# Context's modulation vectors on GpSimd, a third pair by seven products, one vector in the second mixer

## The chip, the cores and the metric

The kernel runs on one core of a Trainium2 chip. PE is the matrix engine, DVE the vector engine, ACT the scalar engine, POOL is GpSimd, and SP is the queue that issues most DMAs. The metric is the device time of one execution in microseconds. Before the change it is 2030.13 us (median of three runs, 2025.8 to 2033.44).

## The reference, cut to what matters

Two layers run over 256 latent tokens and 256 context tokens of width 1024:

```
m  = (silu(c)     @ w_ada[l] + b_ada[l])     # nine vectors of 1024 for the latent tokens
mc = (silu(c_ctx) @ w_ada[l] + b_ada[l])     # the same nine for the context
x  = x  + 0.5*m[2] *swiglu(modulate(rms_norm(x),  m[0],  m[1]),  w1, w3, w2)    # first FFN
y  = token_mixer(modulate(rms_norm(x), m[3], m[4]), ...);  x = x + m[5]*y
x  = x  + 0.5*m[8] *swiglu(modulate(rms_norm(x),  m[6],  m[7]),  w1, w3, w2)    # second FFN
...                                           # the context stream the same with mc; in the last
                                              # layer it ends after the first FFN
swiglu(h, w1, w3, w2) = (silu(h @ w1) * (h @ w3)) @ w2                           # hidden width 2816
```

## The kernel before

**Products.** Activations lie with channels on the 128 partitions and tokens along the row, latent in columns 0 to 255 and context in 256 to 511. Each fp32 operand is split into two fp32r halves (`split_act`: ACT copies the high half, DVE subtracts it for the low half), and three matmuls (high x high, high x low, low x high) make one product. `load_raw` brings 128x1024 floats of weights into a ring `wr` of five tiles.

**An FFN over both streams** (`ffn_both`, called three times: layer 0 twice, layer 1 once) takes the hidden width in eleven pairs of 256 channels. An ordinary pair is four units (two halves of w1, two of w3), each 24 matmuls of 512 columns. A pair "by seven products" (`seven`) has seven units of 24 matmuls of 256 columns, on sums of blocks of weights and of activations; `Forms` makes the sums of activations. Its tiles `s1` and `s3` are each loaded by SP and then added to by a second, accumulating DMA that POOL issues (L759). Pair 0 comes with the handover from the stage before, pairs 1 and 2 are ordinary, 3 to 10 go by seven. Behind pairs 3, 7 and 10 stand the down-projections of what is finished, in units of up to 24 matmuls of 512 columns.

**The order** on PE, DVE and ACT is the order of the code (`pipeline`): at each unit the evacuations of the unit before, the weight split of the unit three ahead, then the unit's matmuls. POOL and SP are ordered by the scheduler. A queue that waits holds up all behind it.

**The modulation vectors** (`ada`) are made beside this: one step loads 128x1024 of `w_ada` into the ring and adds it, times a scalar per partition, to two accumulators in one tile `aacc`, for the latent and the context stream, both on DVE (L238 the first step, L240 the others). After eight steps `ada_end` sums over partitions on PE (`pa`, L255), copies to `mrow` on DVE, transposes on PE (L262) and adds the bias. There is one tile `aacc`, so the first step of a vector waits until PE has read the one before. `pipeline` spreads the steps by each unit's `cost`: 1 for the ordinary units of pair 2, 1 at one unit of a pair by seven, 0.22 per four-row block of the down-projections. One vector, (1,7), goes another way: `ada_apart` multiplies by `w_ada` on PE in the third of these FFNs (L279), between ordinary units. In the mixers and the last FFN the steps are taken by `tick` and `background`.

Of the kernel before, what the change touches and what calls it, by code (L numbers as in the profile page):

```python
# [17 lines left out]
P = 128  # L18
# [61 lines left out]
def dit_kernel(ctx: ExitStack, tc: tile.TileContext, I: dict, out: bass.AP):  # L80
# [146 lines left out]
    def ada(mods, pool, made=None):  # L227
# [22 lines left out]
    def ada_end(l, m, acc, pool):  # L250
# [3 lines left out]
        for q in range(4):  # L254
            te.matmul(pa[32 * q:32 * q + 32, 0, :], ones32, acc[:, q % 2, (q // 2) * 512:(q // 2 + 1) * 512],  # L255
                      start=True, stop=True, tile_position=(0, 32 * q))
# [11 lines left out]
        modulated(l, m)  # L268

    def ada_apart(l, m, pool, made):  # L270

        pa = psum_bg(f"pa{l}_{m}")
        v.memset(pa[:, 0, 0:L], 0.0)
        ahead = ada_load(l, m, 0)
        yield
        for k in range(KD):
            w, ahead = ahead, ada_load(l, m, k + 1) if k + 1 < KD else None
            for q in range(4):
                te.matmul(pa[32 * q:32 * q + 2, 0, 0:L], cs[:, k], w[:, q * L:(q + 1) * L],  # L279
                          start=(k == 0), stop=(k == KD - 1), tile_position=(0, 32 * q))  # L280
            if k == KD - 1:
                made.append(ada_apart_end(l, m, pa, pool))
            yield

    def ada_apart_end(l, m, pa, pool):
        mrow = pool.tile([P, 512], F32, tag="mrow", name="mrow")[:, 0:L]
        v.tensor_copy(mrow, pa[:, 0, 0:L])
        yield
        for b in range(2):
            te.transpose(pa[:, 1, b * P:(b + 1) * P], mrow[:, b * P:(b + 1) * P], ident)  # L290
        yield
        v.tensor_tensor(modT[l][:, m].rearrange("p (q b) t -> p q b t", q=4),
                        pa[:, 1, 0:L].rearrange("p (b q r) -> p q b r", b=2, q=4)[:, :, :, 0:2],
                        biasT[l][:, 8 * m:8 * m + 8].rearrange("p (q b) -> p q b", q=4).unsqueeze(3)
                        .to_broadcast([P, 4, 2, 2]), ALU.add)
        modulated(l, m)
# [353 lines left out]
    def pipeline(units, fills, steps, total, made, apart):  # L650
# [17 lines left out]
        with tc.manual_schedule(engines={eng.PE, eng.DVE, eng.Activation}):  # L668
            for i in range(len(units) + 1):
                prev = units[i - 1] if i else None  # L670
                if prev:
                    if prev.need is not None:
                        while did < prev.need and step():
                            did += 1
                        finish(True)
# [19 lines left out]
                if i < len(units):  # L695
                    want += units[i].cost * scale
                    while did < min(total, int(want + 1e-6)) and step():
                        did += 1
                    for _ in range(2):
                        next(apart, None)  # L700
# [5 lines left out]
    class Forms:  # L706


        def __init__(self, norm, fp):
# [8 lines left out]
            t.append(fp.tile([P, 2, D], F32, tag="aacc", name="ft")[:, 0].rearrange("p (k n) -> p k n", k=4))  # L718

            def whole(o, a, b):  # L720
                v.tensor_tensor(o, a.bitcast(F32), b.bitcast(F32), ALU.add)

            def neg(a, b):
# [848 lines left out]
```

## Time and profile before

| | |
|---|---|
| median of three runs | 2030.13 us |
| the profiled execution's own time | 2027.78 us |
| its span | 2025.9 us |
| PE busy | 1943.0 us (96%) |
| DVE busy | 1556.6 us (77%) |
| ACT busy | 965.5 us (48%) |
| POOL busy | 117.6 us (6%) |
| mean granted clock of PE | 0.982 |

Shares are means over stages with different limits. A DVE busy for 77% of the span can still be the last to be ready in one stage, so the stages are read one by one.

### The profile page before, as it was taken

What the parts mean: (1) busy time and instruction counts of PE and PEld (TensorE: products, weight loads), DVE (VectorE), ACT (ScalarE), POOL (GpSimd) and SP (SyncE); (2) the same over time, 40 slices, a digit from 0 to 9 for tenths busy, and PEclk for the clock granted to TensorE, in tenths of its full rate; (3) what the DMA queues carried; (4) which work ended last, traced back from release to release, by engine and by line L of the source; (5) the groups of instructions that cost most, each with busy time, mean ns of one, the idle gap of its engine ahead of it and who ended that gap; (6) DMA issues with size and microseconds to landing.
All of it is one profiled execution on the core that took longest, in us unless ns stands there. A gap on an engine that the chain in (4) does not pass through costs nothing. (4 is left out here: it accounts for less than half of the span.)

```text
span 2025.9 us, 32128 instructions
## 1 busy us (share of the span) xinstructions
PE 1943.0 (96%) x12797; PEld 1730.5 (85%) x12797; DVE 1556.6 (77%) x2323; ACT 965.5 (48%) x1466; POOL 117.6 (6%) x80
## 2 busy tenths in 40 slices
PE   7999999999999999999999989999999998999998
PEld 5879988898777778888998986889888997899998
DVE  6788778876688878687887866787788779878755
ACT  4434424465566533542533552334244668665444
POOL 2100100000001110100100010001000001210000
PEclk8999999999999999999999999999999999999999
DMA  8866765532213545666775466667655124465763
GB/s 304 218 197 174 200 198 136 154 104 68 89 48 94 172 134 183 157 178 177 195 220 146 136 171 190 190 171 204 198 136 154 57 74 144 145 211 179 239 194 109
DMA packets 278541, 326.48 MB, mean 161 GB/s; under 512 B 15520, under 2 KB 260344, under 8 KB 278136
## 3 DMA queue, kind: packets, MB, share of 16 engines
q1 hardware_dynamic: 253048, 299.27, 47.3%
q0 software_dynamic: 25344, 25.17, 8.4%
q8 instruction: 100, 1.64, 0.3%
q14 instruction: 49, 0.40, 0.1%
HBM read 321.25 MB, written 3.15 MB: 160 GB/s over the span
## 5 line engine op out<-in xcount | busy, mean ns | idle before, releaser
L354 ACT CAST whi<-wraw 128x1024 fp32r<-128x1024 f32 (+2 forms) x371 | 369.9, 1001 | 545.1 <-PE py L350 192.4
L355 DVE TENSOR_TENSOR wlo<-wraw,whi 128x1024 fp32r<-128x1024 f32 (+2 forms) x343 | 402.3, 1176 | 159.4 <-ACT whi L354 154.5
L240 DVE SCALAR_TENSOR_TENSOR aacc<-wada,cs,aacc 128x1024 f32<-128x1024 f32 x210 | 264.6, 1298 | 1.7 <-DMA wada<-w_ada 1.7
L785 PE MATMUL p<-hhi_f,whi 128*128 128x256 f32 x768 | 219.1, 285 | 12.2 <-DVE half L793 12.2
L349 PE MATMUL p<-hhi_f,whi 128*128 128x256 f32 (+1 forms) x672 | 216.9, 323 | 2.4 <-DVE hhi_f L422 2.4
L351 PE MATMUL p<-hhi_f,wlo 128*128 128x256 f32 (+1 forms) x672 | 214.8, 320 | 3.1 <-DVE wlo L355 2.6
L785 PE MATMUL p<-hlo_f,whi 128*128 128x256 f32 x768 | 217.7, 284 | 0.0
L785 PE MATMUL p<-hhi_f,wlo 128*128 128x256 f32 x768 | 217.6, 283 | 0.0
L350 PE MATMUL p<-hlo_f,whi 128*128 128x256 f32 (+1 forms) x672 | 215.5, 321 | 0.5 <-DVE hlo_f L427 0.2
L785 PE MATMUL p<-zone,whi 128*128 128x256 f32 x1152 | 207.4, 283 | 0.5 <-ACT half L790 0.5
L349 PE MATMUL py<-ghi,whi 128*128 128x512 f32 x492 | 193.9, 394 | 0.0
L351 PE MATMUL py<-ghi,wlo 128*128 128x512 f32 x492 | 192.9, 392 | 0.0
L350 PE MATMUL py<-glo,whi 128*128 128x512 f32 x492 | 192.9, 392 | 0.0
L785 PEld LDWEIGHTS p<-zone,whi 128*128 128x128 f32 x1152 | 178.6, 191 | 0.7 <-ACT half L790 0.7
L785 PEld LDWEIGHTS p<-hhi_f,whi 128*128 128x128 f32 x768 | 147.7, 192 | 18.0 <-DVE half L793 15.2
L785 PE MATMUL p<-zone,wlo 128*128 128x256 f32 x576 | 162.4, 282 | 0.0
L785 PEld LDWEIGHTS p<-hhi_f,wlo 128*128 128x128 f32 x768 | 148.9, 194 | 0.0
L785 PEld LDWEIGHTS p<-hlo_f,whi 128*128 128x128 f32 x768 | 148.2, 193 | 0.2
L349 PEld LDWEIGHTS p<-hhi_f,whi 128*128 128x128 f32 x672 | 128.0, 190 | 17.3 <-issue 5.7
L351 PEld LDWEIGHTS p<-hhi_f,wlo 128*128 128x128 f32 x672 | 128.0, 190 | 14.3 <-DVE wlo L355 3.0
L350 PEld LDWEIGHTS p<-hlo_f,whi 128*128 128x128 f32 x672 | 128.3, 191 | 11.5 <-DVE hlo_f L427 1.8
L349 PE MATMUL pg<-hhi_m,whi 128*128 128x512 f32 (+1 forms) x384 | 132.1, 344 | 0.0
(370 smaller groups left out, 4370.9 us busy)
## 6 DMA issues: line engine op xcount, KB each, us to landing
wraw<-ffn_w SPq DMA_DIRECT2D x232, 512.0 KB, 4.6
wada<-w_ada SPq DMA_DIRECT2D x128, 512.0 KB, 3.6
wraw<-w_in SPq DMA_DIRECT2D x64, 512.0 KB, 3.5
s<-ffn_w SPq DMA_DIRECT2D x48, 512.0 KB, 4.8
s<-ffn_w POOLq DMA_DIRECT2D x48, 512.0 KB, 6.3
wraw<-w_out SPq DMA_DIRECT2D x16, 512.0 KB, 3.3
wada<-w_ada SPq DMA_DIRECT2D x30, 256.0 KB, 5.6
wraw<-w_in SPq DMA_DIRECT2D x16, 384.0 KB, 3.7
```

What stands on the lines that cost most here:

```text
L240: v.scalar_tensor_tensor(acc[:, t], w, cs[:, k, t:t + 1], acc[:, t], op0=ALU.mult, op1=ALU.add)
L349: te.matmul(o, a, xh, start=start, stop=False)
L350: te.matmul(o, a, xl, start=False, stop=False)
L351: te.matmul(o, b, xh, start=False, stop=stop)
L354: s.copy(hi, src)
L355: eng.tensor_tensor(lo, src, hi.bitcast(F32), ALU.subtract)
L785: te.matmul(om, wt[w][:, k, cm], form[f][:, k], start=(first and k == m == n == 0), stop=(k == 3 and m == 1 and n == 2), skip_group_check= ...
```

## The change

Each step's context half moves to POOL: a multiply in place on the weight tile, then an add into an accumulator; the two streams have a tile each, `aacc0` and `aacc1`. Pair 2 also goes by seven products, with two of the sums of activations made on POOL. The steps are spread anew: none at the ordinary pair, up to two at a unit of the later ones, and none that begins a vector while the last one's `ada_end` is unfinished. `ada_apart` is gone, and (1,7) is made in the second mixer. Every other group of a down-projection takes its bank from the second ring of PSUM.

```diff
             if k == 0:
-                acc = pool.tile([P, 2, D], F32, tag="aacc", name="aacc")
-            for t in range(2):
+                acc = [pool.tile([P, D], F32, tag=f"aacc{t}", name=f"aacc{t}") for t in range(2)]
+            for t, eng in enumerate((v, gp)):
                 if k == 0:
-                    v.tensor_scalar_mul(acc[:, t], w, cs[:, k, t:t + 1])
+                    eng.tensor_scalar_mul(acc[t], w, cs[:, k, t:t + 1])
+                elif t == 0:
+                    eng.scalar_tensor_tensor(acc[t], w, cs[:, k, t:t + 1], acc[t], op0=ALU.mult, op1=ALU.add)
                 else:
-                    v.scalar_tensor_tensor(acc[:, t], w, cs[:, k, t:t + 1], acc[:, t], op0=ALU.mult, op1=ALU.add)
+                    eng.tensor_scalar_mul(w, w, cs[:, k, t:t + 1])
+                    eng.tensor_tensor(acc[t], acc[t], w, ALU.add)
...
-    def ada_apart(l, m, pool, made):
...
                     want += units[i].cost * scale
-                    while did < min(total, int(want + 1e-6)) and step():
-                        did += 1
-                    for _ in range(2):
-                        next(apart, None)
+                    if units[i].cost:
+                        for _ in range(2):
+
+                            if did < min(total, int(want + 1e-6)) and not (made and did % KD == 0) and step():
+                                did += 1
                     units[i].mm(units[i].w)
...
             self.fills = {
-                1: [lambda: whole(t[0], h11, l11), lambda: whole(t[1], h12, l12)],
-                2: [lambda: whole(t[2], h22, l22), lambda: v.tensor_tensor(t[0], t[0], t[1], ALU.subtract),
+                1: [lambda: whole(t[2], h22, l22, gp), lambda: whole(t[0], h11, l11), lambda: whole(t[1], h12, l12)],
+                2: [lambda: v.tensor_tensor(t[0], t[0], t[1], ALU.subtract),
...
-                4: [lambda: neg(t[0], t[2]), lambda: whole(t[1], h21, l21)],
-                5: [lambda: split_act(z[0][:, 1], z[1][:, 1], t[0]), lambda: neg(t[0], t[1])],
-                8: [lambda: split_act(h12, l12, t[0])]}
+                4: [lambda: whole(t[1], h21, l21, gp), lambda: neg(t[0], t[2]),
+                    lambda: split_act(z[0][:, 1], z[1][:, 1], t[0])],
+                5: [lambda: neg(t[0], t[1])],
+                6: [lambda: split_act(h12, l12, t[0])]}
...
-                        more = {"cost": 1 if c > 1 else 0}
+                        more = {"cost": 0}
...
-                        x["py"] = psum("py")
+                        x["py"] = psum_bg("py") if cg % 2 else psum("py")
...
-                    more = {"cost": 0.22 * n}
+                    more = {"cost": 0.25 * n}
...
-            units = ordinary(1) + ordinary(2)
-            for c0, c1 in ((3, 4), (4, 8), (8, 11)):
-                g0 = 0 if c0 == 3 else c0
+            units = ordinary(1)
+            for c0, c1 in ((2, 4), (4, 8), (8, 11)):
+                g0 = 0 if c0 == 2 else c0
                 for c in range(c0, c1):
-                    units += seven(fm, w1, w3, c * 2 * P, fp, to(c - g0))
+                    units += seven(fm, w1, w3, c * 2 * P, fp, to(c - g0), 1.0 if c < 4 else 0.6)
...
-            pending[:] = [ada(mods, mp)]
...
             with tc.tile_pool(name=f"mm{l}", bufs=1) as mm:
+                pending[:] = [ada(mods, mm)]
...
-    ffn_both(1, 0, entry, [(1, m) for m in range(3, 7)], after, False, (1, 7))
+    ffn_both(1, 0, entry, [(1, m) for m in range(3, 7)], after, False)
     entry = ffn_entry(1, 1, L)
-    mixer(1, L, after, [], entry)
+    mixer(1, L, after, [(1, 7)], entry)
```

Of the seven units of a pair, the third now has cost 1, and the fourth, fifth and last 1.0 (pairs 2 and 3) or 0.6.

On DVE, where in the first FFN modulation vector 4 closes and vector 5 begins (`aacc`, `aacc0` the accumulators, `wlo` splits of weights, `half` sums of weights), before:

```order
L772 TENSOR_TENSOR half1_617<-s1_2511,wraw_2514 128x1024
L238 TENSOR_SCALAR aacc_2635<-wada_2596,cs_116 128x1024 x2
L355 TENSOR_TENSOR wlo_2664<-half1_617,whi_2663 128x1024
L240 SCALAR_TENSOR_TENSOR aacc_2635<-wada_2633,cs_116,aacc_2635 128x1024 x2
L577 SCALAR_TENSOR_TENSOR xT_112<-py_2638,gmod0_123,xT_112 128x256 x4
L355 TENSOR_TENSOR wlo_2708<-wraw_2555,whi_2707 128x1024
L355 TENSOR_TENSOR wlo_2744<-s3_2516,whi_2743 128x1024
L772 TENSOR_TENSOR half0_616<-half1_617,wraw_2555 128x1024
L259 COPY mrow_2748<-pa0_4_2711 128x512
L355 TENSOR_TENSOR wlo_2776<-half0_616,whi_2775 128x1024
```

And after:

```order
L262 COPY mrow_2922<-pa0_4_2886 128x512
L770 TENSOR_TENSOR half0_618<-p3_2826,half0_618 128x512
L330 TENSOR_TENSOR wlo_2952<-wraw_2816,whi_2951 128x1024
L770 TENSOR_TENSOR half1_619<-p1_2825,half1_619 128x512
L330 TENSOR_TENSOR wlo_2987<-s1_2813,whi_2986 128x1024
L749 TENSOR_TENSOR half1_619<-s1_2813,wraw_2816 128x1024
L267 TENSOR_TENSOR modT0_117<-pa0_4_2886,biasT0_118 128x16
L187 SCALAR_TENSOR_TENSOR amod0_121<-modT0_117,colT_115 128x16
L770 TENSOR_TENSOR w1_620<-p3_2826,w1_620 128x512
L330 TENSOR_TENSOR wlo_3019<-half1_619,whi_3018 128x1024
L238 TENSOR_SCALAR aacc0_3025<-wada_2780,cs_116 128x1024
```

Before, the next vector's first step (L238, two instructions) stands ahead of the last one's copy out of `pa` (L259), and splits stand behind it; after, it stands behind the last one's bias (L267), and each step is one instruction.

On POOL, in the same FFN around the pairs 4 to 8 (`s1`, `s3` the accumulating loads, `aacc1` the context's accumulator), before:

```order
L759 DMA s1_1283<-ffn_w3 128x4x256
L759 DMA s3_1288<-ffn_w1 128x4x256
L759 DMA s1_1471<-ffn_w3 128x4x256
L759 DMA s3_1476<-ffn_w1 128x4x256
L759 DMA s1_1698<-ffn_w3 128x4x256
```

And after:

```order
L242 TENSOR_SCALAR wada_1677<-wada_1677,cs_116 128x1024
L243 TENSOR_TENSOR aacc1_1470<-aacc1_1470,wada_1677 128x1024
L736 DMA s1_2038<-ffn_w3 128x4x256
L736 DMA s3_2043<-ffn_w1 128x4x256
L242 TENSOR_SCALAR wada_1775<-wada_1775,cs_116 128x1024
L243 TENSOR_TENSOR aacc1_1470<-aacc1_1470,wada_1775 128x1024
L736 DMA s1_2626<-ffn_w3 128x4x256
L736 DMA s3_2631<-ffn_w1 128x4x256
L242 TENSOR_SCALAR wada_1914<-wada_1914,cs_116 128x1024
L243 TENSOR_TENSOR aacc1_1470<-aacc1_1470,wada_1914 128x1024
```

Before, POOL had nothing but the loads' issues there; after, two instructions of each step stand among them, before and behind issues that wait for a load to land.

## Rows read from the trace of the kernel before

**Rows 1.** Stretches of the three FFNs; columns: us, engines' busy us, PEclk, DMA share, GB/s

```profile
101.06:174.26 73.20, 68.83 (x374) 59.22 (x372) 63.49 (x107) 22.39 (x25) 3.48 (x3) 0.95 0.65 187
174.26:261.18 86.92, 83.41 (x686) 82.17 (x684) 68.58 (x72) 44.38 (x52) 9.71 (x8) 0.96 0.80 199
193.30:212.30 19.00, 19.00 (x163) 19.00 (x162) 17.04 (x17) 10.39 (x13) 2.59 (x2) 1.00 0.80 207
261.18:304.79 43.61, 43.61 (x194) 35.87 (x193) 31.69 (x36) 9.57 (x10) 1.29 (x1) 1.00 0.61 184
304.79:370.39 65.60, 60.62 (x517) 59.59 (x517) 54.98 (x59) 31.53 (x38) 1.30 (x1) 0.97 0.50 133
887.24:953.08 65.84, 65.03 (x373) 56.31 (x372) 54.18 (x59) 21.33 (x23) 2.87 (x3) 1.00 0.67 192
953.08:1039.05 85.97, 82.40 (x686) 81.28 (x685) 69.44 (x72) 43.32 (x51) 9.50 (x8) 0.98 0.79 195
1082.66:1148.63 65.97, 61.00 (x517) 59.96 (x517) 54.97 (x59) 31.52 (x38) 1.56 (x2) 0.95 0.50 132
1269.40:1340.14 70.74, 67.25 (x374) 57.58 (x372) 53.30 (x57) 21.21 (x23) 2.80 (x3) 0.95 0.65 182
1340.14:1425.44 85.30, 81.75 (x686) 80.51 (x685) 68.12 (x73) 42.48 (x50) 9.46 (x7) 0.98 0.79 197
1469.06:1536.39 67.33, 62.36 (x518) 61.32 (x517) 55.00 (x59) 31.70 (x38) 1.45 (x2) 0.97 0.48 130
```

**Rows 2.** Timeline of PE, first FFN, pair 3; columns: start, length, engine, line

```profile
122.67 0.28 PE L785 MATMUL p<-hlo_f,whi 128*128 128x256 f32 x1
...
125.05 0.28 PE L785 MATMUL p<-hlo_f,whi 128*128 128x256 f32 x1
```

**Rows 3.** Timeline of DVE, first FFN, where vector 4 closes

```profile
296.73 1.22 DVE L772 TENSOR_TENSOR half<-s,wraw 128x1024 f32<-128x1024 f32 x1
...
305.93 1.42 DVE L238 TENSOR_SCALAR aacc<-wada,cs 128x1024 f32<-128x1024 f32 x2 [7.98 <-PE pa L255]
...
308.39 2.47 DVE L240 SCALAR_TENSOR_TENSOR aacc<-wada,cs,aacc 128x1024 f32<-128x1024 f32 x2
...
315.76 0.68 DVE L259 COPY mrow<-pa 128x512 f32<-128x512 f32 x1
```

**Rows 4.** Timeline of PE, the same place

```profile
304.79 1.06 PE L255 MATMUL pa<-aacc,ones 128*32 128x512 f32 x8
...
316.50 1.10 PE L262 MATMUL pa<-k_ident,mrow 128*128 128x128 f32 x4 [4.97 <-DVE mrow L259]
```

**Rows 5.** Instructions grouped by line and form, DVE; idle time before them and its releaser

```profile
L238 DVE TENSOR_SCALAR aacc<-wada,cs 128x1024 f32<-128x1024 f32 x30 | 21.9, 766 | 44.9 <-PE pa L255 44.4 <-DMA wada<-w_ada 0.5
```

**Rows 6.** Timeline of POOL: the start, and the first mixer

```profile
16.25 4.66 POOL L355 TENSOR_TENSOR wlo<-wraw,whi 128x1024 fp32r<-128x1024 f32 x2 [15.81 <-ACT whi L354]
...
755.35 2.21 POOL L355 TENSOR_TENSOR wlo<-wraw,whi 128x768 fp32r<-128x768 f32 x1 [15.54 <-ACT whi L354]
```

**Rows 7.** Timeline of DVE beside the second of them

```profile
753.39 6.45 DVE L240 SCALAR_TENSOR_TENSOR aacc<-wada,cs,aacc 128x1024 f32<-128x1024 f32 x4
```

**Rows 8.** Stretches: two FFN beginnings, the mixers' ends, the last FFN's beginning

```profile
824.90:887.24 62.34, 62.27 (x340) 53.38 (x339) 48.05 (x58) 29.06 (x42) 4.71 (x4) 1.00 0.59 146
1194.60:1269.40 74.80, 69.09 (x405) 54.97 (x403) 48.65 (x60) 29.02 (x42) 4.98 (x4) 0.95 0.62 172
690.00:810.00 120.00, 118.39 (x544) 93.83 (x543) 94.73 (x121) 47.26 (x67) 8.77 (x4) 1.00 0.55 172
1750.00:1840.00 90.00, 88.23 (x744) 85.45 (x745) 69.29 (x136) 58.84 (x101) 9.66 (x6) 1.00 0.55 170
1840.00:1890.00 50.00, 47.42 (x397) 46.08 (x395) 47.15 (x56) 29.09 (x40) 0.00 (x0) 0.97 0.76 238
```

**Rows 9.** DMA issues of the profile page; KB each, us to landing

```profile
s<-ffn_w SPq DMA_DIRECT2D x48, 512.0 KB, 4.8
s<-ffn_w POOLq DMA_DIRECT2D x48, 512.0 KB, 6.3
```

More of the change, by code (lines that the diff above doesn't have):

```diff
@@ L254, in ada_end @@
         for q in range(4):
-            te.matmul(pa[32 * q:32 * q + 32, 0, :], ones32, acc[:, q % 2, (q // 2) * 512:(q // 2 + 1) * 512],
+            te.matmul(pa[32 * q:32 * q + 32, 0, :], ones32, acc[q % 2][:, (q // 2) * 512:(q // 2 + 1) * 512],
                       start=True, stop=True, tile_position=(0, 32 * q))
@@ L267, in ada_end @@
                         .to_broadcast([P, 2, 4, 2]), ALU.add)
-        modulated(l, m)
-    def ada_apart(l, m, pool, made):
[L272 to L295, printed above, removed]
         modulated(l, m)
@@ L648, in __init__, with pipeline @@
             self.now, self.end, self.cost, self.need = now, end, cost, need
-    def pipeline(units, fills, steps, total, made, apart):
+    def pipeline(units, fills, steps, total, made):
         eng = mybir.EngineType
@@ L672, in pipeline @@
                     if prev.need is not None:
-                        while did < prev.need and step():
-                            did += 1
+                        assert did >= prev.need, did
                         finish(True)
@@ L706, in dit_kernel, with __init__ @@
     class Forms:
-        def __init__(self, norm, fp):
+        def __init__(self, norm, spare, first):
             hi, lo = norm.hi, norm.lo
@@ L717, in __init__, with whole @@
             t = [x[:, 0:D].rearrange("p (k n) -> p k n", k=4) for x in self.half]
-            t.append(fp.tile([P, 2, D], F32, tag="aacc", name="ft")[:, 0].rearrange("p (k n) -> p k n", k=4))
-            def whole(o, a, b):
-                v.tensor_tensor(o, a.bitcast(F32), b.bitcast(F32), ALU.add)
+            t.append(spare)
+            def whole(o, a, b, eng=v):
+                eng.tensor_tensor(o, a.bitcast(F32), b.bitcast(F32), ALU.add)
             def neg(a, b):
@@ L736, in __init__ @@
             self.n = 0
+            self.sums = [first] * 2 + self.half
         def places(self):
@@ L743, in sum_place, with seven @@
             self.n += 1
-            return self.half[self.n % 2][:, 0:D].rearrange("p (k n) -> p k n", k=4)
-    def seven(fm, wa, wb, c0, fp, done):
+            return self.sums[self.n - 1 if self.n < 3 else 2 + self.n % 2][:, 0:D].rearrange("p (k n) -> p k n", k=4)
+    def seven(fm, wa, wb, c0, fp, done, cost):
         x = {}
@@ L809, in gate @@
             return f
-        cost = 0
         return [
-            Unit(part("b", fm.b11, True), whole("a11"), first_loads, 1, 0, [keep("q1", "b")], cost=cost),
-            Unit(part("c", fm.t1, True), whole("s1"), None, 0, 0, [keep("p5", "c")], cost=cost),
+            Unit(part("b", fm.b11, True), whole("a11"), first_loads, 1, 0, [keep("q1", "b")], cost=0),
+            Unit(part("c", fm.t1, True), whole("s1"), None, 0, 0, [keep("p5", "c")], cost=0),
             Unit(part("b", fm.t2), whole("s2"), None, 0, 1, [keep("w1", "b")], cost=1, first=summed("s2", "s1", "a11")),
@@ L817, in seven @@
             Unit(part("b", fm.t3), whole("s3"), None, 0, 0, [add("p5", "b")], cost=cost),
-            Unit(part("c", fm.b22), whole("s4"), None, 0, 1, [add("w1", "c")], [silu(1, "w1")], cost=cost,
+            Unit(part("c", fm.b22), whole("s4"), None, 0, 1, [add("w1", "c")], [silu(1, "w1")], cost=0,
                  first=summed("s4", "s2", "a12")),
@@ L821, in seven, with ffn_both @@
                  [lambda: done(x["gt"])], cost=cost)]
-    def ffn_both(l, f, norm, mods, then, first, extra=None):
+    def ffn_both(l, f, norm, mods, then, first):
         hhi, hlo = norm.hi, norm.lo
@@ L916, in down @@
                 elif late:
-                    us[0].now, us[0].need = [late[0][0]], late.pop()[1]
+                    us[0].now, us[0].need = [f for f, _ in late], late[0][1]
+                    late.clear()
                 return us
@@ L925, in ffn_both @@
             to(0)(gt)
-            fm = Forms(norm, fp)
-            units = ordinary(1) + ordinary(2)
-            for c0, c1 in ((3, 4), (4, 8), (8, 11)):
-                g0 = 0 if c0 == 3 else c0
+            fm = Forms(norm, fp.tile([P, D], F32, tag="aacc0", name="ft").rearrange("p (k n) -> p k n", k=4),
+                       fp.tile([P, D], F32, tag="aacc1", name="fs"))
+            units = ordinary(1)
+            for c0, c1 in ((2, 4), (4, 8), (8, 11)):
+                g0 = 0 if c0 == 2 else c0
                 for c in range(c0, c1):
-                    units += seven(fm, w1, w3, c * 2 * P, fp, to(c - g0))
+                    units += seven(fm, w1, w3, c * 2 * P, fp, to(c - g0), 1.0 if c < 4 else 0.6)
                 for cg in range(4 if c1 < KF // 2 else 3):
-                    units += down(cg, 2 * g0, 2 * (c1 - g0), c1 == KF // 2, KD if first and cg == g0 == 0 else None)
+                    units += down(cg, 2 * g0, 2 * (c1 - g0), c1 == KF // 2, KD if first and g0 == 0 and cg < 2 else None)
             made = []
             with norm.done():
-                pipeline(units, fm.fills, ada(mods, fp, made), KD * len(mods), made,
-                         ada_apart(*extra, fp, made) if extra else iter(()))
+                pipeline(units, fm.fills, ada(mods, fp, made), KD * len(mods), made)
             for _ in to_residual(w2, 6, (g["hi"], g["lo"]), NTOK, gate, st, fp, weight_places, 16, then, (3,)):
```

1 line of the change is left out of this document (removed).

## Prediction

> **What bounds the kernel now.** I read the table of busy time first: PE at 96% is the bound of the whole. Then I cut each FFN into stretches and compared each with what PE needs there bare [rows 1]. A unit of seven products starts a matmul every 0.113 us (21 starts in 2.38 us [rows 2]), so 168 make a pair in 19.05 us. 192 matmuls of 512 columns take 43.61 us without a gap [rows 1], so 0.227 us each, and an ordinary pair's 96 take 21.8. Allowing 1.5 us for a vector's own matmuls and transposes, bare need and loss are:
>
> - pair 3 and the first down-projection, 19.05 + 43.6 + 1.5 = 64.2: they took 73.20, 65.84 and 70.74, a loss of 9.0, 1.7 and 6.6;
> - the run of pairs 4 to 7, 76.2 + 1.5 = 77.7: 86.92, 85.97, 85.30, a loss of 9.2, 8.3, 7.6;
> - pairs 8 to 10, 57.15 + 1.5 = 58.65: 65.60, 65.97, 67.33, a loss of 7.0, 7.3, 8.7.
>
> Together 65 us. The timelines say why. DVE sat idle for 7.98 us ahead of a vector's first step, because there is one `aacc` and PE had not read the last one [rows 3]; the splits queued behind came late, the copy to `mrow` ended at 316.4, and PE stood 4.97 us before its transposes [rows 4]. Over the kernel DVE waited 44.4 us in this way [rows 5]. Part of the loss is clock: in the runs the granted clock is 0.95 to 0.98, beside 1.00 in the down-projection [rows 1]. Only then did I look at DVE's load. In an undisturbed stretch of a run it is busy 17.04 of 19.00 us, one two-instruction step included [rows 1]. It is nearly a second bound there, so what the change does to DVE decides.
>
> **The parts of the change.**
>
> Pair 2 by seven products: 3 x (21.8 - 19.05) = 8 us less on PE.
>
> `ada_apart` goes: the beginning of the third FFN, which has it, took 74.80 us, the same stretch of the second 62.34 [rows 8]. That is 12.5 us, less about 1.4 that the vector costs PE in the second mixer (one `pa` of 1.06 us [rows 4] and four transposes of 128 columns): 11 us.
>
> The wait for `aacc` goes: by the order a new vector's first step now stands behind the old one's bias, so nothing on DVE waits there for PE's reading. What is late next is DVE itself, and POOL.
>
> A step on DVE: before, two instructions, 2.47 us, 2.4 without their overlap with the next [rows 3]. After, one, 1.2. On POOL an add of 128x1024 takes 2.33 (two in 4.66, started ahead of DVE's [rows 6]). The multiply is in no row. It lies between DVE's 0.77 for the same shape [rows 5] and POOL's add; I take 1.3, half of the add for its one operand and a little fixed cost. So POOL works 3.63 us for a step.
>
> That isn't free for DVE. In the first mixer four such instructions on DVE took 6.45 us [rows 7] where 4 x 1.2 + 0.07 = 4.87 would do, and it is in there that POOL's subtraction of 2.21 us ran [rows 6], which alone takes some 1.84 (three quarters of 2.33 and a fixed cost). DVE lost 1.58 of these 1.84: 0.86, with all its operands in SBUF and no gap. In a run it is busy 0.90 of the time, and of a pair's 17 us some 2.5 read PSUM (three adds and a gate). If reads of PSUM don't collide, 0.86 x 0.90 x 0.85 = 0.66 of POOL's work is lost to DVE. I take 0.70, since POOL's part of a step starts right behind DVE's. The ends are 0 and 1. A step then costs DVE 1.2 + 0.7 x 3.63 = 3.75 us, and not 2.4: more than before.
>
> The Trainium skill, "SBUF — State Buffer", section "Who interferes with whom", says that a DVE instruction with two SBUF inputs and a GpSimd instruction that reads SBUF exclude each other: whoever issues first gets the shared ports for the whole instruction, the other blocks fully. The pair of rows agrees. By it alone the share would be 1, which is the second rival's far end.
>
> The Trainium skill, "GPSIMD Engine Reference", section "Engine selection", has one-input work on GpSimd at roughly line rate, an estimate of 0.85 us for the multiply at its 1.2 GHz. With that the sum below would come to 1990 us; no row shows it.
>
> The runs, by DVE. By the order, 7 steps fall into pairs 4 to 7, 6 into 8 to 10 and 5 into 2 and 3. A pair without steps costs DVE 17.04 - 2.4 = 14.6. A run adds 1 us for `mrow` and bias and 2 to 2.5 for waits on ACT's casts (2 us of 19 were idle). Splits are made three units ahead, 8.2 us of PE, less one unit's DVE work of 2.4: PE can bear 5.8 us of lag.
>
> - Pairs 4 to 7: 58.4 + 26.2 + 3.5 = 88.1 against 77.7 + 5.8: loss 4.6.
> - Pairs 8 to 10: 43.8 + 22.5 + 3 = 69.3 against 64.45: 4.9.
> - Ordinary pair, 2 and 3: DVE has 47.4 (6.8 + 29.2, and ten instructions of 1.14 for the sums of activations), 3.3 for two sums that POOL makes, 18.8 for steps: 69.5 against 59.9 + 5.8: 3.8. The first FFN also carries the mixers' scalars; it lost 7.4 more there than the second, of which I keep 6.
> - First down-projection: 2, since the transposes stand right behind `pa` in the first two FFNs.
>
> That is 3 x 15.3 + 6 = 52 us in place of 65: 13 us saved. The other down-projections stay at no loss: of 43.6 us DVE is busy 31.7 with some eight old steps in them [rows 1], and six new ones cost it less than 23.
>
> The mixers and the last FFN: there 32 steps are done, 8 of them new. At 0.62, for DVE reads PSUM more there, a step costs 3.45. That is 24 x 1.05 + 8 x 3.45 = 53 us more of DVE's time, in stretches where it is busy 94.73 of 120, 69.29 of 90 and 47.15 of 50 [rows 8]. Its slack of 25, 21 and 3 us and the lead hide most; I take 4, 5 and 3 = 12 us, from ends of 0 and 53.
>
> The sum: -8 - 11 - 13 + 12 = -20 us on the profiled 2027.78, which lies 0.1% under the median, less than a measurement tells: 2008 us. About 0.5%, 10 us, is what a measurement of this kernel can tell from no change.
>
> What is queued behind POOL's new waits: its multiply waits for the weight tile and for DVE's read of it, and behind it in POOL's order stand the accumulating loads of `s1` and `s3`, for which the splits wait. A tile of `wr` is held by some 5 us more, and SP's loads wait for it. I count this as covered by the lead, since POOL stays under half busy in a run (7 x 3.63 + 8 x 1.3 us of issuing in 82).
>
> **The rivals.**
>
> 1. The exclusion bites less: share 0.5, if POOL's work falls into DVE's gaps. A step costs 3.0, the runs come to 82.9 and 64.8 and lose next to nothing, the FFNs lose 13 in all, and the rest costs 7: 1964 us. For it: DVE is idle for 0.1 of a run. Against it: rows 7.
>
> 2. It bites harder, and DVE becomes the bound: slower. At 0.86 in the runs too, a step costs 4.3; the losses are 8.6, 8.3, 7.3 and 2 per FFN, 85 with the scalars, so 19 more than before; -8 - 11 + 19 + 18 (mixers and last FFN at the same share) = +18: 2046 us. At 1 it is 2081. The point from which the change is a loss is a share of 0.79, or a multiply of 1.75 us at 0.7. For it: a run has 17 instructions per pair with hardly a gap, so POOL always finds one to hold up.
>
> 3. POOL's order: two vectors per FFN close inside a run, and PE's `pa` now needs POOL's last add too, 3.6 us behind DVE's, and more if an accumulating load stands ahead that waits for its first part to land (4.8 us [rows 9]). If all six are late by that, PE loses 29 us and the gain is gone: 2036 us, or about 2025 if half are. Against it: two or three units, 5.4 to 8.2 us, lie between.
>
> **How the numbers follow.** Forecast, 1990 to 2017 us: 0.42. Rival 1: 0.12. Rival 3 at half, no change to be told: 0.18. Rival 2, and rival 3 in full: 0.28. So faster 0.54, same 0.18, slower 0.28. The range goes from 1970, short of rival 1, to 2058, past rival 2 at 0.86; the forecast's own is 1990 to 2017.
>
> **What would show it.** DVE's adds and subtractions of 128x1024 (1.22 us) would show means of 1.5 to 1.9 us in the runs, each stretched one beside a POOL instruction; POOL's multiply some 1.3 and add over 2.33. The waits at L238 for `pa` would be gone from DVE, and PE's waits in the runs be short ones for `wlo`, at a clock of 1.00. Runs of pairs 4 to 7 would take 81 to 84 us, 8 to 10 some 63. The beginning of the third FFN would take no longer than the second's. The forecast is wrong if a run takes 86 or more, or if PE's longest idle time ends on POOL.

## The result, and the profile after

The changed kernel takes 2246.7 us (median of 3, 2245.2 to 2252.9) where the kernel before takes 2030.1: a ratio of 1.108, 95% interval 1.103 to 1.112. The forecast of 2008 us is 239 too low, and the time lies far above its range.

The page of the changed kernel: busy time, then the costliest POOL groups (line engine op, out<-in, form, count | busy us, mean ns | idle time before and its releaser); L242 is the multiply of a step, L243 its add.

```profile
PE 1995.9 (89%) x12959; PEld 1762.4 (78%) x12959; DVE 1633.3 (73%) x2231; ACT 972.2 (43%) x1487; POOL 868.6 (39%) x332
...
L242 POOL TENSOR_SCALAR wada<-wada,cs 128x1024 f32<-128x1024 f32 x112 | 385.9, 3446 | 219.2 <-DVE aacc L240 216.7
L243 POOL TENSOR_TENSOR aacc<-aacc,wada 128x1024 f32<-128x1024 f32 x112 | 306.3, 2734 | 8.7
```

No engine is full: PE stands idle for 11% of a longer span, and DVE, the feared second bound, has 73%. POOL's multiply takes 3.45 us in the mean, and 2.84 at the least (the row below), not 1.3; with the add a step takes POOL 6.2 us, not 3.63. The multiply's own durations (min/median/max in ns):

```profile
L242 POOL TENSOR_SCALAR wada<-wada,cs x112: 2837/3400/4891, 105.1 to 2104.6; 128x1024 f32<-128x1024 f32 x112
```

The stretches that answer to [rows 1] and [rows 8], columns as there: the three runs of pairs 4 to 7, pairs 8 to 10 of the first FFN, and the end of the first mixer.

```profile
193.94:297.16 103.22, 86.10 (x685) 82.01 (x684) 75.86 (x68) 40.96 (x50) 54.08 (x24) 0.92 0.70 179
1068.06:1170.89 102.83, 85.29 (x685) 81.19 (x684) 76.22 (x68) 40.54 (x50) 53.26 (x24) 0.93 0.71 179
1477.37:1586.45 109.08, 84.94 (x687) 81.06 (x686) 77.76 (x73) 40.33 (x49) 62.26 (x24) 0.91 0.68 174
340.68:414.67 73.99, 64.74 (x517) 60.82 (x516) 58.58 (x54) 30.79 (x38) 36.49 (x13) 0.95 0.47 132
780.00:820.00 40.00, 18.69 (x65) 13.60 (x63) 14.22 (x11) 6.74 (x8) 36.20 (x13) 0.76 0.43 135
820.00:860.00 40.00, 32.50 (x122) 24.82 (x123) 25.81 (x25) 9.08 (x11) 34.07 (x12) 0.81 0.38 119
```

A run of pairs 4 to 7 takes 103 to 109 us in place of 85 to 87, with DVE busy for 0.71 to 0.74 of it. In the first 40 us shown of the mixer DVE is busy for 14 us and PE for 19, while POOL is busy for 36: of the three only POOL is nearly full there, and the granted clock is 0.76. That POOL's steps make this loss h2 shows further down.

Who waits for whom (engine and line that wait, engine and line waited for: us in total, times, longest); first PE, then SP's queue and ACT, each of these two with its counterparts before:

```profile
PE pa L258 <- POOL aacc L243: 58.5, 12, 10.8
PE p L762 <- DVE half L770: 30.5, 23, 6.6
PE p L762 <- ACT half L767: 22.3, 14, 2.9
PE pg L324 <- ACT whi L329: 21.9, 4, 10.4
```

```profile
SPq L302 <- POOL aacc L243: 439.2, 69, 11.5
SPq L224 <- POOL aacc L243: 284.9, 43, 9.5
```

Before:

```profile
SPq L327 <- DVE aacc L240: 159.5, 49, 5.5
SPq L224 <- DVE aacc L240: 128.6, 44, 6.1
```

ACT after, then before:

```profile
ACT whi L329 <- DMA wraw<-ffn_w: 90.1, 28, 10.7
ACT whi L329 <- DMA wraw<-w_in: 59.3, 16, 10.3
```

```profile
ACT whi L354 <- DMA wraw<-ffn_w: 37.2, 22, 4.0
ACT whi L354 <- DMA wraw<-w_in: 1.8, 2, 1.1
```

DVE's 44.4 us of waits at a vector's first step [rows 5] are gone, as foretold. In their place PE waits for POOL's last add. SP's loads wait 724 us for POOL to give back a tile of `wr`, where before they waited 288 us for DVE's last use of one. And weights land later: ACT, which casts them, waits 149 us for these two transfers, and before it waited 39. One such place, the timeline of POOL and then PE where vector 4 closes in the first FFN, answering to [rows 3, 4]:

```profile
257.75 1.30 POOL L736 DMA_DIRECT2D s<-ffn_w  x1 [5.59 <-DVE half L770]
258.54 3.88 POOL L242 TENSOR_SCALAR wada<-wada,cs 128x1024 f32<-128x1024 f32 x1
262.50 2.34 POOL L243 TENSOR_TENSOR aacc<-aacc,wada 128x1024 f32<-128x1024 f32 x1
264.83 2.84 POOL L242 TENSOR_SCALAR wada<-wada,cs 128x1024 f32<-128x1024 f32 x1
267.75 2.34 POOL L243 TENSOR_TENSOR aacc<-aacc,wada 128x1024 f32<-128x1024 f32 x1
```

```profile
258.63 1.04 PE L258 MATMUL pa<-aacc,ones 128*32 128x512 f32 x2
270.14 1.93 PE L258 MATMUL pa<-aacc,ones 128*32 128x512 f32 x6 [10.46 <-POOL aacc L243]
```

An accumulating load stands ahead of two steps on POOL and is itself held up by DVE; POOL begins the vector's last two steps when PE already wants their sum.

### The profile page after: what moved, and what is told of

Read it like the earlier page. It is cut to its first block, busy times and chain, and to the rows that moved or that the text cites. A ratio compares the mean times of both kernels' runs of the same rounds, so it can differ in the third digit from the quotient of the medians.

```text
span 2251.2 us, 32808 instructions
## 1 busy us (share of the span) xinstructions
PE 1995.9 (89%) x12959; PEld 1762.4 (78%) x12959; DVE 1633.3 (73%) x2231; ACT 972.2 (43%) x1487; POOL 868.6 (39%) x332
## 5 line engine op out<-in xcount | busy, mean ns | idle before, releaser
L330 DVE TENSOR_TENSOR wlo<-wraw,whi 128x1024 fp32r<-128x1024 f32 (+2 forms) x340 | 450.7, 1329 | 240.0 <-ACT whi L329 232.6
L242 POOL TENSOR_SCALAR wada<-wada,cs 128x1024 f32<-128x1024 f32 x112 | 385.9, 3446 | 219.2 <-DVE aacc L240 216.7
L243 POOL TENSOR_TENSOR aacc<-aacc,wada 128x1024 f32<-128x1024 f32 x112 | 306.3, 2734 | 8.7
L330 POOL TENSOR_TENSOR wlo<-wraw,whi 128x768 fp32r<-128x768 f32 (+2 forms) x28 | 53.1, 1898 | 543.3 <-ACT whi L329 496.0
L736 POOL DMA_DIRECT2D s<-ffn_w x54 | 71.1, 1317 | 381.2 <-DMA s<-ffn_w 93.0
L324 PE MATMUL py<-ghi,whi 128*128 128x512 f32 x492 | 196.0, 398 | 16.7 <-ACT ghi L329 16.7
L240 DVE SCALAR_TENSOR_TENSOR aacc<-wada,cs,aacc 128x1024 f32<-128x1024 f32 x112 | 184.6, 1648 | 35.7 <-DMA wada<-w_ada 35.3
L762 PEld LDWEIGHTS p<-hhi_f,whi 128*128 128x128 f32 x864 | 166.3, 192 | 40.6 <-DVE half L770 34.0
L324 PE MATMUL p<-hhi_f,whi 128*128 128x256 f32 (+1 forms) x576 | 179.5, 312 | 6.0 <-ACT whi L329 3.6
L762 PEld LDWEIGHTS p<-hlo_f,whi 128*128 128x128 f32 x864 | 166.2, 192 | 0.3
L762 PEld LDWEIGHTS p<-hhi_f,wlo 128*128 128x128 f32 x864 | 166.4, 193 | 0.0
```

The lines of the kernel that those rows point to most:

```text
L240: eng.scalar_tensor_tensor(acc[t], w, cs[:, k, t:t + 1], acc[t], op0=ALU.mult, op1=ALU.add)
L242: eng.tensor_scalar_mul(w, w, cs[:, k, t:t + 1])
L243: eng.tensor_tensor(acc[t], acc[t], w, ALU.add)
L324: te.matmul(o, a, xh, start=start, stop=False)
L330: eng.tensor_tensor(lo, src, hi.bitcast(F32), ALU.subtract)
L736: gp.dma_start(t, rowsof(second[0], 4 * second[1], 4, c0, 2 * P), accum_op=ALU.add)
```

## The experiments

Theories: **A**, POOL's instructions hold up DVE, and the multiply is longer than assumed; **B**, POOL is late and PE waits at `pa`; **C**, the other edits cost; **D**, POOL holds the weight tiles. The kernel before took 2025.3 to 2026.3 us beside these runs. Stretches in us, read from the starts of PE's matmuls in the profiled executions (F1 to F4 the FFNs, M0 and M1 the mixers, in order of time; single executions, so a few us are noise):

```
                        F1     M0     F2     F3     M1     F4
before                 346.8  421.1  357.2  387.7  247.6  213.4
after                  391.3  476.8  398.8  413.7  287.4  231.4
e1 both on DVE         350.3  422.7  361.8  385.0  264.2  214.1
e3 unread              366.3  476.0  378.8  401.9  284.4  233.9
f1 no step on POOL     335.2  419.8  347.0  363.5  257.9  211.8
f3 vector back         349.3  423.3  361.4  398.8  247.5  219.2
g1 own tile, in pace   353.4  477.2  362.7  378.5  281.3  220.0
h1 POOL in FFNs        384.8  426.9  393.8  418.4  267.8  214.6
h2 POOL in mixers      350.3  472.8  361.7  381.2  286.4  231.9
```

### POOL or the rest: e1, e2

e1, against the changed kernel:

```diff
-            for t, eng in enumerate((v, gp)):
+            for t, eng in enumerate((v, v)):
...
-                elif t == 0:
+                else:
                     eng.scalar_tensor_tensor(acc[t], w, cs[:, k, t:t + 1], acc[t], op0=ALU.mult, op1=ALU.add)
-                else:
-                    eng.tensor_scalar_mul(w, w, cs[:, k, t:t + 1])
-                    eng.tensor_tensor(acc[t], acc[t], w, ALU.add)
```

> The changed kernel, with the context stream's part of each step back on DVE as one instruction (acc = w*c + acc); everything else of the change stays: accumulators apart, pair 2 by seven products, the steps' new spread, the vector in the second mixer. Theory A (POOL's multiply, 2.84 us at the least and 3.45 in the mean instead of 1.3, makes a step on POOL 6.2 us, and this work holds up DVE) and theory B (POOL is late, and PE waits at pa for its last add): both 1985 to 2015 us, below the kernel before, since -8 for pair 2, -11 for ada_apart and part of the -13 for the aacc waits remain. Theory C (the other edits, not POOL, cost most of it): above 2100.

2054.4 us, ratio 1.014 (1.011 to 1.018). Its busy times:

```profile
PE 1932.9 (94%) x12959; PEld 1726.8 (84%) x12959; DVE 1601.1 (78%) x2359; ACT 974.1 (48%) x1487; POOL 144.0 (7%) x92
```

e2 is the kernel before with the steps on POOL as in the change, and with the two accumulators apart that they need:

```diff
-            for t in range(2):
+            for t, eng in enumerate((v, gp)):
...
+                    eng.tensor_scalar_mul(w, w, cs[:, k, t:t + 1])
+                    eng.tensor_tensor(acc[t], acc[t], w, ALU.add)
```

> The kernel before with one edit: two accumulators apart and the context stream's part on POOL (multiply in place, add). The old spread of the steps, pair 2 in the ordinary form and ada_apart stay. A and B: 2210 to 2290, for POOL's part of the change is then worth more than the whole of it. C: below 2090.

2218.1 us, ratio 1.094 (1.089 to 1.099). POOL's part costs 192 us on either ground. PE's waits aren't all of it: PE is busy for 1995.9 us in the changed kernel and for 1932.9 in e1 with the same 12959 matmuls, at a mean granted clock of 0.949 against 0.988, so that 63 of the 201 us between these two profiled executions are matmuls that took longer. But e1 missed its ranges too: the rest doesn't gain what pair 2 and the vector were to give (19 us), it loses 28. So A or B holds in the main, and C in part.

### What POOL's part is made of: e3, e4, f1, f2, g1

In e3 every `pa` matmul reads `acc[0]`.

```diff
-ones32, acc[q % 2][:, (q // 2) * 512:(q // 2 + 1) * 512],
+ones32, acc[0][:, (q // 2) * 512:(q // 2 + 1) * 512],
```

> The changed kernel, but the sum over partitions reads the first accumulator for both streams, so that nobody waits for POOL's accumulator (this leaves the context stream's modulation out of the result). POOL's instructions are all there. A (DVE loses time to POOL's work, and the waits at pa are only one place where the delay shows): 2200 to 2247. B (PE waits at pa for POOL, 127.9 us of idle time before L258 on PE and its weight loads, some of it counted on both): 2120 to 2185.

2202.4 us, 1.087 (1.083 to 1.091): the reading costs 44 of the 192. So B's mechanism is real, but most of the loss has another cause.

e4:

```diff
-                    eng.tensor_scalar_mul(w, w, cs[:, k, t:t + 1])
```

> The changed kernel without POOL's multiply: POOL adds the weight tile as it is (this leaves out the scaling of the context stream's sums). POOL's part of a step falls from 6.2 us to some 2.4, below the 3.63 that the forecast assumed. If the size of the multiply is what was wrong, this should come out at or below the forecast's 2008 by the same working: a step on DVE 1.2 + 0.7 x 2.34 = 2.84 us in place of 3.75: 1960 to 2010. If POOL's place in the order costs, whatever its instructions take (two waits a step, accumulating loads behind them): 2100 or more.

2133.5 us, 1.054 (1.050 to 1.057). POOL's steps take 364 us in place of 740 and cost 79 over e1 in place of 192. But at 2.8 us a step, below the forecast's 3.63, the kernel is still 125 us above the forecast's 2008: the multiply's length alone is not the error.

f1 is e3 without the context stream's instructions. f2 is e3 with them on a tile of their own (the first of a vector a memset):

```diff
...
-                    eng.tensor_scalar_mul(w, w, cs[:, k, t:t + 1])
-                    eng.tensor_tensor(acc[t], acc[t], w, ALU.add)
...
+                    gp.tensor_scalar_mul(acc[1], acc[1], cs[:, k, 1:2])
+                    gp.tensor_tensor(acc[1], acc[1], acc[1], ALU.add)
```

> The changed kernel with the context stream's steps left out, on POOL and everywhere else; the sum over partitions reads the first accumulator for both streams (this leaves the context stream's modulation out of the result). It is the ground level for the next run: 2000 to 2035 us by every theory, for DVE has 128 x 1.25 = 160 us less to do than with both streams on it (2054) and nobody waits for POOL.

1990.8 us, 0.983 (0.982 to 0.985), below its range. Its busy times:

```profile
PE 1919.9 (97%) x12959; PEld 1723.5 (87%) x12959; DVE 1464.8 (74%) x2231; ACT 977.4 (49%) x1487; POOL 138.2 (7%) x92
```

> As the run before, but POOL does a multiply in place and an add of 128x1024 for each step but a vector's first on a tile of its own, which nobody reads: POOL waits for no weight tile, holds none, and no one waits for its end. (The context stream's modulation is left out of the result.) Theory A (POOL's instructions hold up DVE's while they run): 2130 to 2180, most of what is left with nobody waiting for POOL (2202). Theory D (the weight tiles are held until POOL's multiply and add are through, so that SP's loads come late; SP's queue waited 724 us for POOL's last use of a tile in the changed kernel): within 25 us of the run before, 2010 to 2060.

2267.3 us, 1.119 (1.117 to 1.122), outside both ranges and more than with all the waits. PE's longest waits, and POOL's timeline towards the end of the first run of pairs 4 to 7, say why:

```profile
PE p L761 <- ACT whi L328: 118.1, 3, 42.9
```

```profile
263.46 2.85 POOL L241 TENSOR_SCALAR aacc<-aacc,cs 128x1024 f32<-128x1024 f32 x1
266.39 1.89 POOL L242 TENSOR_TENSOR aacc<-aacc 128x1024 f32<-128x1024 f32 x1
268.23 1.32 POOL L735 DMA_DIRECT2D s<-ffn_w  x1
```

POOL's order isn't written out, a scheduler makes it; with nothing to wait for, the steps of a whole FFN went ahead of the accumulating loads, and PE stood three times for some 40 us until they came. This run measures POOL's order, not A. g1 mends that: each of POOL's steps takes its scalar from a column that DVE copies behind its own part of the step. Against f2:

```diff
...
+            v.tensor_copy(ticket[:, k:k + 1], cs[:, k, 1:2])
...
-                gp.tensor_scalar_mul(acc[1], acc[1], cs[:, k, 1:2])
+                gp.tensor_scalar_mul(acc[1], acc[1], ticket[:, k:k + 1])
```

> As f2, but each of POOL's steps on its own tile takes its scalar from a column that DVE copies (one element per partition) right behind its own part of the step. In f2 nothing held POOL's steps back, and they stood in a heap ahead of its accumulating loads (three stalls of PE, 37.05, 43.20 and 38.70 us). With the column POOL works where it does in the changed kernel, but holds no weight tile, and nobody reads its result. (The context stream's modulation is left out.) Theory A (DVE is held up while POOL runs): 2120 to 2180, most of what e3 lost (2202, against 1991 with no step on POOL). Theory D (weight tiles held too long): 1990 to 2040.

2133.1 us, 1.053 (1.050 to 1.056). So from 1991 us, POOL's work on a tile of its own costs 142, weight tiles held by POOL some 69 more (e3's 2202), the reading at `pa` 44 (2247). The 69 isn't the tiles alone: in g1 the add reads one tile twice and takes 1.89 us where e3's takes 2.34, each at the least, and DVE makes 128 copies of 0.15 us more. A and D both have a part; but by the table 57 and 23 of the 142 arise in the mixers, and there g1 loses as much as e3, so that the 69 arises in the FFNs. Two of PE's waits in the mixers, in the second and the first:

```profile
PE pb L328 <- POOL wlo L332: 18.3, 1, 18.3
PE pg L326 <- DVE gt L1407: 17.3, 1, 17.3
```

The splits of the mixers' branch weights are POOL's, and stand between the steps in its queue; DVE in turn waited 16 us for POOL to read its column, a wait that only g1 has. Which of the mixers' waits weighs most isn't told apart: in g1 PE has four stalls of 14 to 18 us, in the changed kernel it waits for late weights and at `pa`.

### Stretch by stretch, and the multiply's size: h1, h2, h3

```diff
-            for t, eng in enumerate((v, gp)):
+            for t, eng in enumerate((v, gp if made is not None else v)):
...
-                elif t == 0:
+                elif eng is v:
```

That is h1 (`made` is a list in the first three FFNs alone); h2 has `made is None`.

> The changed kernel with POOL taking the context stream's steps in the first three FFNs alone; in the mixers and the last FFN both streams are on DVE. By the stretches of the profiles (changed kernel against both on DVE) POOL costs 41, 37 and 29 us in the three FFNs, and 54, 23 and 17 in the two mixers and the last FFN. Theory P (the losses are made where POOL works, each stretch by itself: in the FFNs by the reading at pa, the tiles of wr and DVE, in the mixers by the splits of the branch weights that stand in POOL's own queue): 2054 + 107 = 2145 to 2180. Theory Q (a common cause, such as DVE's lost time adding up from stretch to stretch, or the lower clock of the whole): below 2110 or above 2200.

2164.7 us, 1.069 (1.066 to 1.072): +110.

> The other half: POOL takes the context stream's steps in the mixers and the last FFN alone (32 of the 128), both streams on DVE in the first three FFNs. Theory P: 2054 + 95 = 2130 to 2165, some 3 us for each POOL step, because 16 of them stand close together in the first mixer, where POOL also splits the branch weights. If DVE's lost time were the price, 32 steps would cost a quarter of the 192 us: 2095 to 2110.

2138.6 us, 1.055 (1.052 to 1.057): +84. The two add up to 195, the whole of 192, and the table has the losses where POOL works: P holds. Of the 84 the table puts 50 into the first mixer, 22 into the second and 18 into the last FFN. A POOL step in the mixers and the last FFN costs 2.6 us of the kernel's time, one in the first three FFNs 1.2. The first mixer's end in h2 (columns as in [rows 1]) shows POOL nearly full and DVE half idle:

```profile
720.00:760.00 40.00, 26.35 (x103) 20.05 (x101) 28.13 (x19) 8.72 (x10) 37.61 (x13) 0.83 0.29 95
760.00:800.00 40.00, 28.25 (x118) 21.17 (x118) 15.80 (x16) 7.99 (x9) 30.72 (x12) 0.87 0.38 126
```

h3:

```diff
-                    eng.tensor_scalar_mul(w, w, cs[:, k, t:t + 1])
+                    eng.tensor_scalar_mul(w[:, 0:D // 2], w[:, 0:D // 2], cs[:, k, t:t + 1])
```

> The changed kernel with POOL's multiply on the first 512 of the 1024 columns (the other half of the context stream's sums goes without its scaling). The multiply then takes some 1.45 us alone, near the 1.3 of the forecast. If the duration of the multiply is all that was wrong, this comes out at the forecast plus what the other runs showed beside it (25 for the new spread, some 11 for the vector): 2030 to 2060. If the loss grows with the work on POOL from the add upwards (2133 without a multiply, 2247 with a whole one): 2175 to 2205.

2178.5 us, 1.076 (1.073 to 1.078).

```profile
L242 POOL TENSOR_SCALAR wada<-wada,cs x112: 1552/1572/3595, 105.5 to 2032.2; 128x512 f32<-128x512 f32 x112
```

With a multiply of 1.57 us alone (2.11 in the mean) the loss is 68 us less and still 124 over e1. The forecast's sum doesn't hold with a multiply of its own size.

### The rest: f3, f4, g2, g3, g4, h4

f3 is e1 with the vector (1, 7) back on PE:

```diff
...
-    ffn_both(1, 0, entry, [(1, m) for m in range(3, 7)], after, False)
+    ffn_both(1, 0, entry, [(1, m) for m in range(3, 7)], after, False, (1, 7))
...
-    mixer(1, L, after, [(1, 7)], entry)
+    mixer(1, L, after, [], entry)
```

> The kernel with both streams on DVE (2054 us), with the vector (1, 7) moved back out of the second mixer to the matmuls on PE in the third FFN. If the forecast's step holds (ada_apart gone gives 11 us): 2060 to 2070. If the vector costs the second mixer as much as it cost the third FFN (the stretch from the end of the third FFN to the end took 17 us more with it than before): 2040 to 2054.

2054.0 us, 1.015 (1.012 to 1.017), e1's time. The table has both sides: with the vector back the third FFN takes 13.8 us more and the second mixer 16.7 less; the last FFN took 5 more.

f4 is e1 with pair 2 ordinary. Its forms were still made at the changed kernel's units, partly over data that pair 2 has yet to read, so that its result and its waits differ; g4 below asks again.

```diff
-            units = ordinary(1)
-            for c0, c1 in ((2, 4), (4, 8), (8, 11)):
+            units = ordinary(1) + ordinary(2)
+            for c0, c1 in ((3, 4), (4, 8), (8, 11)):
...
```

> The kernel with both streams on DVE (2054 us), with pair 2 in the ordinary form again (its units take a step each, as before, and the sums go to the two half tiles as before). If the forecast's step holds (pair 2 by seven products gives 8 us): 2058 to 2068. If DVE cannot follow two pairs by seven products with the forms' own sums and five steps in them (the stretch to the end of pair 3 took some 8 us more than its bare need in each of the three FFNs): 2030 to 2042.

2070.0 us, 1.022 (1.019 to 1.025). Not used further.

g2 is e1 with the old spread:

```diff
...
-units += seven(fm, w1, w3, c * 2 * P, fp, to(c - g0), 1.0 if c < 4 else 0.6)
+units += seven(fm, w1, w3, c * 2 * P, fp, to(c - g0), 0)
...
-more = {"cost": 0.25 * n}
+more = {"cost": 0.22 * n}
...
-                    if units[i].cost:
-                        for _ in range(2):
...
-                            if did < min(total, int(want + 1e-6)) and not (made and did % KD == 0) and step():
-                                did += 1
+                    while did < min(total, int(want + 1e-6)) and not (made and did % KD == 0) and step():
+                        did += 1
```

> Both streams on DVE, accumulators apart, pair 2 by seven products, the vector in the second mixer, but the steps spread by the costs of the kernel before (units of a pair by seven products cost nothing but the third, 0.22 for a row of the down-projections, no limit of two steps for a unit), and still no new vector while an old one's end is open. If the new spread is what makes both on DVE slower than before (2054 against 2026), by taking steps from the down-projections into the pairs, where DVE is tight: 2005 to 2030. If not: 2045 to 2060.

2029.0 us, 1.0022 (1.0005 to 1.0038): the new spread costs 25. It takes steps out of the down-projections, where DVE has room (31.69 us busy of 43.61 [rows 1]), into the pairs, where it has little: in the first FFN's run of pairs 4 to 7 DVE has 14 instructions of the steps in e1 and 10 in g2, in the down-projection ahead of it 14 and 18.

g3 is the kernel before with the condition alone:

```diff
-while did < min(total, int(want + 1e-6)) and step():
+while did < min(total, int(want + 1e-6)) and not (made and did % KD == 0) and step():
```

> The kernel before with one condition more: no step of a new vector while an old vector's end is still open, so that DVE's first step no longer waits for PE's reading of the only accumulator (44.4 us of DVE's idle time). If these waits cause the loss of the runs as the forecast says, 13 us go: 2008 to 2018. If the loss has other causes (the clock, DVE's load) or comes back elsewhere: 2021 to 2032.

2021.1 us, 0.9978 (0.9960 to 0.9995): 4 us, give or take 4, not 13. The first run, the pairs 8 to 10 behind it, the third run, and the second:

```profile
172.45:253.25 80.80, 80.55 (x686) 79.18 (x685) 67.75 (x71) 43.74 (x51) 9.08 (x7) 1.00 0.83 210
296.87:365.61 68.74, 62.05 (x518) 60.81 (x518) 53.94 (x58) 31.36 (x38) 1.40 (x2) 0.95 0.45 127
1321.12:1411.63 90.51, 81.39 (x686) 79.63 (x685) 79.84 (x84) 42.81 (x51) 9.08 (x7) 0.94 0.80 207
946.07:1026.79 80.72, 80.62 (x686) 79.38 (x685) 68.98 (x72) 43.28 (x51) 9.08 (x7) 1.00 0.82 206
```

The waits were the cause of the first two runs' loss: it falls from 9.2 us to 3.1 and from 8.3 to 3.0, at a clock of 1.00. But the steps come later: the pairs 8 to 10 lose 3 us more than before, and the third run, now with thirteen DVE instructions more than the first (84 against 71), 5 more.

g4 is g2 with f4's edit, a step for each ordinary unit of pair 2, and the forms made and the sums placed as before:

```diff
...
-more = {"cost": 0}
+more = {"cost": 1 if c > 1 else 0}
...
```

> g2 with pair 2 in the ordinary form again (its units take a step each, the forms and sums in the places of the kernel before). If the forecast's step holds, pair 2 by seven products is worth 8 us: 8 us above g2, 2013 to 2040. If DVE has no room for it: at g2's time or up to 10 us below it.

2037.1 us, 1.0061 (1.0030 to 1.0093): 8 us over g2, give or take 7 by the intervals.

h4 is the version to which the parts point: the kernel before with g3's condition and pair 2 by seven products; beside f3, it has g2's spread and the first mixer's steps where they were:

```diff
...
+            pending[:] = [ada(mods, mp)]
...
-                pending[:] = [ada(mods, mm)]
...
```

> A version made of the parts that paid: the kernel before with pair 2 by seven products (8 us, g4 against g2) and the condition of g3 (4 us); both streams on DVE, the steps spread by the old costs, the vector (1, 7) on PE in the third FFN, the first mixer's steps where they were. If the two add up: 2010 to 2017, below both kernels. If the room that pair 2 takes (two sums more on POOL, the banks of the down-projections, the forms made in one pair's time) costs what g2 and g4 lost beside it: 2020 to 2032.

2023.2 us, 0.9984 (0.9971 to 0.9997). It beats the kernel before by 3 us, give or take 3, and not g3 by anything. If pair 2 by itself gains the 8 of g4 against g2, the edits that came with it lose as much; which of them (two sums on POOL, the banks of the down-projections, the earlier forms), no run tells.

## Why the prediction was wrong

**The step that failed** is the one that costed POOL's work. It charged 0.70 of that work to DVE and took everything that waits for POOL as covered: "I count this as covered by the lead, since POOL stays under half busy in a run", and 12 us for mixers and last FFN. Both parts were wrong, in opposite directions: DVE lost a share of 0.23, and POOL's steps cost 192 us (e1, e2) where they were taken as covered.

- *DVE's share.* f1 and the changed kernel have the same 2231 instructions on DVE. It is busy 1464.8 us in the one and 1633.3 in the other: POOL's 740 us of steps took 168 from it, a share of 0.23. A step costs DVE 2.6 us, not 3.75, about what it did before (2.47). The share of 0.86 behind the 0.70 was read beside a subtraction of POOL's, which reads two tiles [rows 6, 7]; it was carried over to the multiply, which is more than half of a step and takes little from DVE (last section). Rival 2, DVE as the bound, did not come; the time is longer than it gave, but for another reason.
- *The cover.* POOL was over half busy in a run (54 of 103 us). The tiles that it holds cost some 69 us (e3 against g1, which also has a shorter add), counted at nothing. Rival 3's mechanism, PE at `pa` behind POOL's last add, was there at 44 us (e3), against 29 at most (of which a half would have made 2022 us, not about 2025).
- *Mixers and last FFN.* POOL's steps alone cost 84 us there (h2 against e1), and the whole term was put at 12. The working looked at DVE's slack there, and not at POOL's: 16 steps of 6.2 us stand in 110 us of the first mixer, beside splits of POOL's own.
- *The multiply.* 2.84 us alone, outside the bounds of 0.77 and 2.33 too. No reason was given why an instruction with one operand could not take longer than one with two. It accounts for 68 us at the least (h3).

The Trainium skill, "SBUF — State Buffer", section "Who interferes with whom", would have made the share 1; the runs do show DVE and POOL holding each other up, but DVE lost no more than 0.52 of POOL's time (e4), and by the trace mostly beside POOL's adds and subtractions (last section). The Trainium skill, "GPSIMD Engine Reference", section "Engine selection", by which the multiply was estimated at 0.85 us, is off by a factor of more than three here: 2.84.

The other terms:

- *Pair 2, -8.* Borne out by g4 against g2 (8, give or take 7); by h4 the edits that came with it take as much again.
- *`ada_apart`, -11.* The third FFN gained 13.8, but the second mixer lost 16.7, not 1.4 and a share of 12: no gain (f3). DVE's slack there was counted as free. Why the vector costs as much there as on PE, no run isolates.
- *The waits for `aacc`, -13.* The cause was right, and so was a gain in the runs (6 and 5 us in two of three, g3). "What is late next" was DVE's later steps: 4 us are left.
- *The spread* had no term of its own and cost 25 (g2). The forecast put the steps in by their number for each run, with DVE's mean load; the limit and the new costs move them to where DVE has least room. The count of 7 steps in a run was the first FFN's: in the third FFN ten steps fall into it.

The sum as the runs have it: from 2026, -8 (pair 2), 0 (the vector), -4 (the condition), +25 (the spread) and some 15 that no run isolates make e1's 2054; +192 for POOL makes the result. The marks that were set beforehand said so at once: runs over 86 us, and PE's largest wait ending on POOL.

## What to carry to other kernels

Work handed to a slow engine costs by its latency, wherever somebody waits for that engine: list the tiles that it holds, the results that are read, and what else stands in its queue, and compare its step with the distance between steps where these are closest, not with the mean. Price an unseen instruction on its own before summing with it, and leave its upper bound open if nothing in the profile bounds it. A stretch that loses to a wait gets back only what the next late thing leaves.

## What the runs showed of the hardware

POOL's multiply by a value for each partition, in place on 128x1024 f32, takes 2.84 us at the least, and 1.55 on 512 columns (h3), so some 2.5 ns a column; its add of two such tiles takes 2.34 at the least. The instruction with one tile to read is the slower.

The multiply holds up DVE little, the add much. Busy times in e4 (POOL has the adds, and the first multiply of each vector):

```profile
PE 1969.8 (92%) x12959; PEld 1759.5 (83%) x12959; DVE 1653.6 (78%) x2231; ACT 973.0 (46%) x1487; POOL 499.9 (23%) x220
```

Against f1 DVE lost 189 us to POOL's 364 of steps, 0.52. With 386 us of multiplies more, in the changed kernel, it lost 168. The changed kernel's trace tells the two apart. Of DVE's additions and subtractions of 128x1024, the 336 that meet no multiply, add or subtraction of POOL's take 1.22 us in the mean; the 111 that start while a multiply of POOL runs take 1.31; the 59 that start while an add or a subtraction of POOL runs take 2.57. For DVE's own step instructions the same three means are 1.28, 1.54 and 2.87. One of each kind, first an add, then a multiply, each with the DVE instruction that starts beside it:

```profile
223.25 3.30 POOL L243 TENSOR_TENSOR aacc<-aacc,wada 128x1024 f32<-128x1024 f32 x1
224.52 3.11 DVE L330 TENSOR_TENSOR wlo<-s,whi 128x1024 fp32r<-128x1024 f32 x1 [0.21 <-ACT whi L329]
237.17 4.00 POOL L242 TENSOR_SCALAR wada<-wada,cs 128x1024 f32<-128x1024 f32 x1
237.24 1.22 DVE L749 TENSOR_TENSOR half<-s,wraw 128x1024 f32<-128x1024 f32 x1
```

DVE's subtraction ended 1.1 us after the add, about its own length; beside the multiply DVE took no longer, and the multiply took 4.00 us in place of 2.84 (3.45 in the mean).

The scheduler's order on POOL depends on what its instructions wait for: without a wait (f2) the kernel is 134 us slower than with one (g1).
